# Delta-rule stage with weights in two split parts, and modulation rows loaded a step ahead of their sums

## The chip, the cores and the metric

The kernel runs on one core of one Trainium2 chip. The metric is the device time of one execution in microseconds (us), the median of several runs.

## What is computed

A sequence of 256 rows of 1024 float32 values goes through two blocks. The first is a state-space block whose normalizations are modulated by rows made from a vector `c`; the second has two layers, one with a gated delta rule and one with gated linear attention, each followed by an MLP. The parts that matter here, cut from the reference:

```python
def adaln(c, w, b):                       # twice: before the mixer and before the feed-forward
    mod = jax.nn.silu(c) @ w + b          # 3 x 1024 values each
    shift, scale, gate = jnp.split(mod, 3, axis=-1)

def _mixer_gdn(h, w_in, conv_w, a_log, dt_bias, norm_g, w_out):     # 8 heads of 128
    proj = jnp.matmul(h, w_in)            # columns: q, k, v, z (1024 each), beta and gate (32)
    qkv = silu(_depthwise_conv(proj[..., :A_CONV_CH], conv_w))      # 5 taps
    q, k = _l2norm(...), _l2norm(...)
    o_f = _gated_delta_chunked(q, k, v, beta[0], g[0])
    o_b = _flip(_gated_delta_chunked(_flip(q), _flip(k), _flip(v), _flip(beta[1]), _flip(g[1])))
    return jnp.matmul(_rmsnorm(o_f + o_b, norm_g) * silu(z), w_out)
```

## The kernel before, in words

All activations are float32. A weight matrix is cut into pieces of 128 x 1024 values (512 KB). SyncE's queue loads each into a buffer of the tag "raw" (six buffers), and `w3` brings it into one of three forms. In form "S" ScalarE writes the high part, rounded to float32r, and VectorE subtracts it from the piece for the low part. In form "D" ScalarE writes the negated rounded piece, a DMA from GpSimd's queue adds the piece to it, which leaves the low part, and ScalarE writes the high part. High and low parts lie in buffers of the tag "w" (eight, so four weights). A split weight takes three float32r products for each k (`mm3`: high by high, high by low, low by high). In form "N" the piece goes to TensorE unsplit, in one float32 product for each k, which the trace shows as two instructions. `self.form` is a string whose letters alternate over the weights: "SDND" in the state-space stage, "SD" for the gates, "S" in most others and "N" in the delta-rule stage (`gdn`). There every second weight is also loaded straight into a "w" buffer (`self.deep`).

The feed-forward before `gdn` ends with a normalization whose rows are transposed by TensorE and, for form "N", copied once into `h2` (`xpose`). `gdn` then runs, in the order of the program: the first half of z (`proj_z(0, True)`, four weights), `small_tok("w_ba")` (one weight, with the gate's softplus behind it), the k projections (`qkv(4 + i)`, two weights each, with a five-tap convolution whose other taps are VectorE's, line 555), the decay matrices (`decay`, whose right-hand sides `sr` also take "w" buffers), the Gram matrices `MT`, eight block copies by ScalarE (line 1199), a forward substitution of 31 steps on VectorE (lines 1255 and 1259), the placement of its result in `C` and `CT` (line 1272), two levels of block products (lines 1285 to 1304), the v and q projections, the products of the two directions (lines 1332 to 1421), and the second half of z (`proj_z(1, False)`). The next stage begins with `w_aout`.

The 48 modulation rows of `adaln` are sums on VectorE: each row of 128 x 1024 weights is loaded into a "raw" buffer and multiplied with `silu(c)` and summed in one instruction (line 452). Sixteen are made at the start. 24 wait in a list, from which `ada_next` takes one in each of four groups of the state-space stage, two after each of eight gate projections and one at each turn in `merge`; the last eight are made in the feed-forward.

The order on each engine is not the order of the program. A planner fixes each engine's instructions ahead of the run, from the program's order as priority and from its own times for when each is ready; buffers of one tag are handed out in turn. At run time each engine goes through its list in order. The 31-tap convolution of the state-space stage (`acc`) has a priority below all else.

Of the kernel before, what the change touches and what calls it, by code (L numbers as in the profile page):

```python
# [18 lines left out]
P = 128  # L19
T = 256  # L20
D = 1024
# [50 lines left out]
NW = 14  # L72
FORM_GDN = "N"

# [41 lines left out]
class K:  # L116
    def __init__(self, ctx, tc, A):
        self.tc, self.nc, self.A = tc, tc.nc, A
        pool = lambda name, **kw: ctx.enter_context(tc.tile_pool(name=name, **kw))
        self.cp = pool("cp", bufs=1)  # L120
        self.px = pool("px", bufs=1)
        self.dp = pool("dp", bufs=1, space=bass.MemoryType.DRAM)
        self.wp = pool("wp", bufs=1)
        self.wx = self.big = self.sm = self.ps = self.kp = None
        self.n = self.nw = 0
        self.pending = None
        self.form = "S"
        self.deep = False

# [31 lines left out]
    def w3(self, name, i, nk, extra=False):  # L161
# [4 lines left out]
        if form == "N":  # L166
            if self.deep and self.nw % 2:
                t = self.wp.tile([P, 1024], F32, tag="w", bufs=8, name=self.nm("wn"))
                nc.sync.dma_start(t, self.A[name][i])
            else:  # L170
                t = self.raw(self.A[name][i])
            return (t.rearrange("p (k c) -> p k c", k=nk),)
# [276 lines left out]
    def ada(self, name, i, mod):  # L449

        w = self.raw(self.A[name][i])
        self.nc.vector.tensor_tensor_reduce(  # L452
            out=w, in0=w, in1=self.sc, scale=1.0, scalar=0.0, op0=ALU.mult, op1=ALU.add,
            accum_out=mod[:, i : i + 1],
        )

    def ada_next(self, n):

        for a in self.waiting[:n]:
            self.ada(*a)  # L460
        del self.waiting[:n]
# [51 lines left out]
    def hsplit(self):  # L513
        t = self.px.tile([P, 2, 2, 8, P], F32R, tag="hh", name=self.nm("hh"))
        return t[:, 0], t[:, 1], None, t

    def h32(self):
        return self.px.tile([P, 2, 2, 8, P], F32, tag="hh", name=self.nm("h32"))[:, 0]

    def xpose(self, src, t, out):  # L520

        nc = self.nc
        for k0 in (0, 4):
            b = self.pS()
            for kk in range(4):
                nc.tensor.transpose(b[:, kk * P : (kk + 1) * P], src[:, (k0 + kk) * P : (k0 + kk + 1) * P], self.ident)
            nc.scalar.copy(out[:, t, k0 : k0 + 4, :], b.rearrange("p (k t) -> p k t", k=4))

# [80 lines left out]
    def state_space(self, h, banks):  # L609
# [70 lines left out]
        for g in range(4):  # L680
# [22 lines left out]
            def ev_z(b):  # L703
                for t in range(2):
                    self.silu2(z[:, t], b[t])

            self.proj_tok("w_z", g, h, ev_z)
            nc.vector.tensor_tensor(
                out=x0s.rearrange("p (h d) -> p h d", h=8),
# [82 lines left out]
    def merge(self, yT, acc, tg):  # L792
# [39 lines left out]
        for i in range(4):  # L832
            self.projA([("w_conv_out", i, ev_c(i))], ch)
            self.ada_next(ADA_PER[3])
        self.ada_next(24)
        self.ada_bias(self.mod2, "b_ada_ffn", 0, 16)
# [82 lines left out]
    def feed_forward(self, mh):  # L919
# [51 lines left out]
        nc.gpsimd.dma_start(wf, self.A["r_final"])  # L971
        h2 = self.h32()

        def norm2(t, b):
            self.residual(t, b, gate2[0])
            y = self.rms_tok(self.x[:, t], wf)
            self.later(t, lambda: self.xpose(y, t, h2))
            nc.gpsimd.dma_start(self.spill[:, t], y)

        self.down("w_ffn_down", 11, hidden, norm2)  # L980
        return None, None, h2

# [75 lines left out]
    def gdn(self, h):  # L1058
# [43 lines left out]

        self.form = FORM_GDN
        self.deep = True
        proj_z(0, True)
# [171 lines left out]
        for hq, l in ((0, 0), (0, 1), (1, 0), (1, 1)):  # L1277
            for t in range(2):
# [25 lines left out]
                nc.vector.copy_predicated(CT[:, gs], mask, wb.rearrange("p (h l) -> p h l", h=4))  # L1304

        for i in range(4):
            vv = self.smt([P, 2, T], "vT")
            qkv(8 + i, vv)
            to_tok(vt, vv, 2 * i)
# [22 lines left out]
        for hq in range(2):  # L1332
# [91 lines left out]
            for t in range(2):  # L1424
# [6 lines left out]
                for hh in range(4):  # L1431
# [3 lines left out]
                    )  # L1435
        self.deep = False
        return self.halves_out(zg)
# [375 lines left out]
```

## Time and profile before

| | |
|---|---|
| median of 3 runs | 1398.12 us |
| lowest and highest | 1397.02 and 1402.75 us |
| the profiled execution's own time | 1398.72 us |
| its span, first to last instruction | 1397.0 us |
| its mean granted TensorE clock | 0.979 |

The profile is one execution. Its rows give busy time, idle time and what ended the idle time (the releaser, inferred from semaphore events). PE is TensorE, PEld its weight loads, DVE VectorE, ACT ScalarE, POOL GpSimd, SP SyncE; L555 is line 555 of the kernel. Matmuls are pipelined, so a row's busy time is longer than the distance from one matmul to the next; distances are read from starts.

### The profile page before, as it was taken

How to read it: one execution, taken by the hardware profiler on the slowest of the kernel's cores; microseconds unless marked ns; L12 is line 12 of the kernel's file. 1: busy time of each engine (PE TensorE's matmuls, PEld its weight loads, DVE VectorE, ACT ScalarE, POOL GpSimd, SP SyncE). 2: the span in 40 equal slices, each digit the busy share in tenths (PEclk: the TensorE clock that was granted, in tenths of full speed). 3: DMA queues.
4: the chain of work that ended last, by engine and by line, in shares of the span. 5: the costliest groups of instructions: out<-in, count | busy, mean ns of one | idle time of the engine just before them, and what ended most of it. 6: DMA issues, size and time to landing. Idle time of an engine off the chain costs nothing. (4 is left out here: it accounts for less than half of the span.)

```text
span 1397.0 us, 19743 instructions
## 1 busy us (share of the span) xinstructions
PE 1308.5 (94%) x7336; PEld 1113.3 (80%) x7336; DVE 1000.3 (72%) x1890; ACT 732.9 (52%) x1309; POOL 98.6 (7%) x115
## 2 busy tenths in 40 slices
PE   5898999889998999998989898999999999899997
PEld 4797888789986888875877776788887987688886
DVE  7989988779467777744479976866575796866564
ACT  4655878655446544524344454555444655555450
POOL 0111101010000000000100531000000000000000
PEclk9999999999899999998999999999999999999999
DMA  9898577799355666535423014856464323676530
GB/s 337 289 258 223 172 199 201 226 297 349 104 199 177 235 220 213 192 151 169 136 69 106 31 61 160 265 193 208 130 205 149 122 71 114 207 238 201 179 122 30
DMA packets 69136, 251.69 MB, mean 180 GB/s; under 512 B 7951, under 2 KB 8079, under 8 KB 68528
## 3 DMA queue, kind: packets, MB, share of 16 engines
q1 hardware_dynamic: 62208, 224.08, 47.8%
q0 software_dynamic: 6832, 26.35, 8.2%
q8 instruction: 57, 0.93, 0.3%
q14 instruction: 39, 0.32, 0.1%
HBM read 232.06 MB, written 2.10 MB: 168 GB/s over the span
## 5 line engine op out<-in xcount | busy, mean ns | idle before, releaser
L185 DVE TENSOR_TENSOR wlo<-raw,whi 128x1024 fp32r<-128x1024 f32 (+1 forms) x200 | 241.2, 1211 | 75.9 <-ACT whi L184 71.8
L184 ACT CAST whi<-raw 128x1024 fp32r<-128x1024 f32 (+1 forms) x200 | 207.4, 1042 | 143.1 <-PE psa L201 42.0
L185 DVE TENSOR_TENSOR xlo<-raw,xhi 128x1024 fp32r<-128x1024 f32 x100 | 122.0, 1223 | 73.6 <-ACT xhi L184 69.7
L184 ACT CAST xhi<-raw 128x1024 fp32r<-128x1024 f32 x100 | 104.9, 1051 | 89.3 <-DMA raw<-in_w_mlp 66.8
L231 PE MATMUL psa<-hh,whi 128*128 128x512 f32 x384 | 136.9, 396 | 0.0
L231 PE MATMUL pss<-hh,whi 128*128 128x512 f32 x384 | 136.4, 396 | 0.0
L200 PE MATMUL psb<-xhi,hid 128*128 128x512 f32 x344 | 135.5, 394 | 0.6 <-ACT hid L375 0.6
L202 PE MATMUL psb<-xhi,hidl 128*128 128x512 f32 x344 | 135.8, 395 | 0.0
L201 PE MATMUL psb<-xlo,hid 128*128 128x512 f32 x344 | 135.5, 394 | 0.0
L202 PE MATMUL psa<-hh,wlo 128*128 128x256 f32 x432 | 125.3, 290 | 6.0 <-DMA wlo<-raw 6.0
L200 PE MATMUL psa<-hh,whi 128*128 128x256 f32 x432 | 126.5, 294 | 4.5 <-DVE c L555 2.5
L201 PE MATMUL psa<-hh,whi 128*128 128x256 f32 x432 | 124.8, 289 | 0.9 <-DVE hh L195 0.9
L232 PE MATMUL psa<-hh,wlo 128*128 128x256 f32 x384 | 107.2, 279 | 0.0
L232 PE MATMUL pss<-hh,wlo 128*128 128x256 f32 x384 | 107.0, 279 | 0.0
L555 DVE SCALAR_TENSOR_TENSOR acc<-u,vecs,acc 128x240 f32<-128x240 f32 (+25 forms) x240 | 100.9, 464 | 0.3
L202 PEld LDWEIGHTS psa<-hh,wlo 128*128 128x128 f32 x432 | 84.7, 196 | 7.6 <-DMA wlo<-raw 6.8
L200 PEld LDWEIGHTS psa<-hh,whi 128*128 128x128 f32 x432 | 84.8, 196 | 6.9 <-ACT hh L194 2.9
L201 PEld LDWEIGHTS psa<-hh,whi 128*128 128x128 f32 x432 | 84.6, 196 | 2.5 <-DVE hh L195 1.9
L231 PEld LDWEIGHTS pss<-hh,whi 128*128 128x128 f32 x384 | 72.1, 188 | 17.1
L231 PEld LDWEIGHTS psa<-hh,whi 128*128 128x128 f32 x384 | 72.0, 188 | 17.0
L452 DVE CUSTOM_DVE_ANT_0 raw<-raw,g 128x1024 f32<-128x1024 f32 x48 | 58.6, 1221 | 30.9 <-DMA raw<-in_w_ada_ffn 18.8
L200 PEld LDWEIGHTS psb<-xhi,hid 128*128 128x128 f32 x344 | 64.4, 187 | 16.6 <-ACT hid L375 1.2
(426 smaller groups left out, 2944.6 us busy)
## 6 DMA issues: line engine op xcount, KB each, us to landing
raw<-in_w_mlp SPq DMA_DIRECT2D x120, 512.0 KB, 4.5
raw<-in_w_ffn_in SPq DMA_DIRECT2D x40, 512.0 KB, 4.4
wlo<-raw POOLq DMA_DIRECT2D x31, 512.0 KB, 6.8
raw<-in_w_ada_mix SPq DMA_DIRECT2D x24, 512.0 KB, 5.3
raw<-in_w_ada_ffn SPq DMA_DIRECT2D x24, 512.0 KB, 4.4
raw<-in_w_ffn_down SPq DMA_DIRECT2D x22, 512.0 KB, 4.4
raw<-in_w_xs SPq DMA_DIRECT2D x16, 512.0 KB, 4.6
raw<-in_w_z SPq DMA_DIRECT2D x16, 512.0 KB, 5.5
```

The costliest lines, as they stand in the source:

```text
L184: nc.scalar.copy(hi, t)
L185: nc.vector.tensor_tensor(out=lo, in0=t, in1=hi.bitcast(F32), op=ALU.subtract)
L200: mm(out, ah, bh, start=start, stop=False)
L201: mm(out, ah, bl, start=False, stop=False)
L202: mm(out, al, bh, start=False, stop=stop)
L231: mm(b, wh[:, k], x[3][:, :, :, k], start=k == 0, stop=False, skip_group_check=True)
L232: mm(b[:, T:], wl[:, k], x[0][:, :, k], start=False, stop=k == 7, skip_group_check=True)
L452: self.nc.vector.tensor_tensor_reduce(out=w, in0=w, in1=self.sc, scale=1.0, scalar=0.0, op0=ALU.mult, op1=ALU.add, accum_out=mod[:, i : i ...
L555: nc.vector.scalar_tensor_tensor(out=o, in0=i, scalar=taps[:, j : j + 1], in1=o, op0=ALU.mult, op1=ALU.add)
```

## The change

In the delta-rule stage the form "N" with its deep loads is gone. Up to the block products the form is "S"; from the v projections on it is "D". As the second half of z is emitted after v and q, its weights are "D" too. The normalized rows ahead of the stage are split into two parts (`xpose_split`), because the split products need them. `ada_next` now sums the rows that the call before it loaded, and then loads the next ones; calls with 0 sum what is loaded and load nothing. The helpers `h32` and `xpose` go.

```diff
--- before.py
+++ after.py
@@ -70,7 +70,7 @@
 FORM_GATES = "SD"
 
 NW = 14
-FORM_GDN = "N"
+FORM_GDN = ("S", "D")
 
 
 def m_lev(l):
@@ -123,9 +123,9 @@
         self.wp = pool("wp", bufs=1)
         self.wx = self.big = self.sm = self.ps = self.kp = None
         self.n = self.nw = 0
+        self.loaded = []
         self.pending = None
         self.form = "S"
-        self.deep = False
 
     def phase(self, name, big, wx, a, b, s):
         return _Phase(self, name, big, wx, a, b, s)
@@ -164,11 +164,7 @@
         self.nw += 1
         form = self.form[self.nw % len(self.form)] if self.nw > NW else "S"
         if form == "N":
-            if self.deep and self.nw % 2:
-                t = self.wp.tile([P, 1024], F32, tag="w", bufs=8, name=self.nm("wn"))
-                nc.sync.dma_start(t, self.A[name][i])
-            else:
-                t = self.raw(self.A[name][i])
+            t = self.raw(self.A[name][i])
             return (t.rearrange("p (k c) -> p k c", k=nk),)
         if extra and self.wx is not None:
             hi, lo = (self.wx.tile([P, 1024], F32R, tag="wx", name=self.nm(v)) for v in ("xhi", "xlo"))
@@ -448,7 +444,9 @@
 
     def ada(self, name, i, mod):
 
-        w = self.raw(self.A[name][i])
+        self.ada_sum(self.raw(self.A[name][i]), i, mod)
+
+    def ada_sum(self, w, i, mod):
         self.nc.vector.tensor_tensor_reduce(
             out=w, in0=w, in1=self.sc, scale=1.0, scalar=0.0, op0=ALU.mult, op1=ALU.add,
             accum_out=mod[:, i : i + 1],
@@ -456,8 +454,9 @@
 
     def ada_next(self, n):
 
-        for a in self.waiting[:n]:
-            self.ada(*a)
+        for a in self.loaded:
+            self.ada_sum(*a)
+        self.loaded = [(self.raw(self.A[name][i]), i, mod) for name, i, mod in self.waiting[:n]]
         del self.waiting[:n]
 
     def ada_bias(self, mod, bname, lo, hi):
@@ -513,18 +512,6 @@
     def hsplit(self):
         t = self.px.tile([P, 2, 2, 8, P], F32R, tag="hh", name=self.nm("hh"))
         return t[:, 0], t[:, 1], None, t
-
-    def h32(self):
-        return self.px.tile([P, 2, 2, 8, P], F32, tag="hh", name=self.nm("h32"))[:, 0]
-
-    def xpose(self, src, t, out):
-
-        nc = self.nc
-        for k0 in (0, 4):
-            b = self.pS()
-            for kk in range(4):
-                nc.tensor.transpose(b[:, kk * P : (kk + 1) * P], src[:, (k0 + kk) * P : (k0 + kk + 1) * P], self.ident)
-            nc.scalar.copy(out[:, t, k0 : k0 + 4, :], b.rearrange("p (k t) -> p k t", k=4))
 
     def xt(self):
         return self.px.tile([P, 2, D], F32, tag="x", name=self.nm("x"))
@@ -705,6 +692,7 @@
                     self.silu2(z[:, t], b[t])
 
             self.proj_tok("w_z", g, h, ev_z)
+            self.ada_next(0)
             nc.vector.tensor_tensor(
                 out=x0s.rearrange("p (h d) -> p h d", h=8),
                 in0=xdt[:, 0].rearrange("p (h d) -> p h d", h=8),
@@ -832,7 +820,8 @@
         for i in range(4):
             self.projA([("w_conv_out", i, ev_c(i))], ch)
             self.ada_next(ADA_PER[3])
-        self.ada_next(24)
+        assert not self.waiting
+        self.ada_next(0)
         self.ada_bias(self.mod2, "b_ada_ffn", 0, 16)
         self.ada_bias(self.mod, "b_ada_mix", 16, 24)
         self.gate1 = self.gate_rows(self.mod, 0.5)
@@ -969,16 +958,16 @@
 
         wf = self.g4()
         nc.gpsimd.dma_start(wf, self.A["r_final"])
-        h2 = self.h32()
+        h2 = self.hsplit()
 
         def norm2(t, b):
             self.residual(t, b, gate2[0])
             y = self.rms_tok(self.x[:, t], wf)
-            self.later(t, lambda: self.xpose(y, t, h2))
+            self.later(t, lambda: self.xpose_split(y, t, h2[0], h2[1]))
             nc.gpsimd.dma_start(self.spill[:, t], y)
 
         self.down("w_ffn_down", 11, hidden, norm2)
-        return None, None, h2
+        return h2
 
 
     def layer_norm(self, gname, i, last=False):
@@ -1100,8 +1089,7 @@
 
             self.proj_tok("w_az", c, h, ev_z, early)
 
-        self.form = FORM_GDN
-        self.deep = True
+        self.form = FORM_GDN[0]
         proj_z(0, True)
         kT = self.bigt([P, 8, T], name="kT")
         qT = self.bigt([P, 8, T], name="qT")
@@ -1303,6 +1291,7 @@
                     nc.tensor.matmul(wb[:, j * P : (j + 1) * P], U[:, j], R2[:, j], start=True, stop=True)
                 nc.vector.copy_predicated(CT[:, gs], mask, wb.rearrange("p (h l) -> p h l", h=4))
 
+        self.form = FORM_GDN[1]
         for i in range(4):
             vv = self.smt([P, 2, T], "vT")
             qkv(8 + i, vv)
@@ -1433,7 +1422,6 @@
                     nc.vector.scalar_tensor_tensor(
                         out=o, in0=o_all[:, t, h0 + hh], scalar=rs[:, hh : hh + 1], in1=o, op0=ALU.mult, op1=ALU.mult
                     )
-        self.deep = False
         return self.halves_out(zg)
 
     def halves_out(self, zg):
```

## Rows read from the trace of the kernel before

**Rows 1.** The page's first part: busy us, share of the span and number of instructions of each engine.

```profile
PE 1308.5 (94%) x7336; PEld 1113.3 (80%) x7336; DVE 1000.3 (72%) x1890; ACT 732.9 (52%) x1309; POOL 98.6 (7%) x115
```

**Rows 2.** Busy time in stretches of the delta-rule stage: window, its length, then PE, PEld, DVE, ACT and POOL busy us with instruction counts, granted TensorE clock, DMA share, GB/s.

```profile
624.00:640.00 16.00, 15.76 (x45) 7.67 (x45) 4.34 (x7) 2.60 (x7) 1.68 (x3) 1.00 0.31 100
640.00:666.00 26.00, 22.31 (x89) 16.62 (x88) 15.31 (x62) 15.88 (x48) 0.00 (x0) 0.81 0.56 189
666.00:703.00 37.00, 35.07 (x191) 30.55 (x191) 15.93 (x46) 14.94 (x27) 7.57 (x6) 1.00 0.35 120
703.00:770.00 67.00, 60.61 (x271) 50.06 (x269) 59.03 (x151) 28.29 (x47) 3.12 (x4) 0.95 0.28 87
770.00:802.00 32.00, 28.59 (x202) 24.61 (x203) 30.00 (x46) 14.45 (x43) 16.28 (x12) 0.95 0.11 34
802.00:847.00 45.00, 41.54 (x290) 35.34 (x289) 30.15 (x69) 26.64 (x87) 14.42 (x14) 1.00 0.18 59
```

**Rows 3.** The timeline of TensorE, in four pairs: split products of 512 columns, split products of 256 columns (in each pair the third product of one k and of the next), unsplit z products (two k of one weight in each row, two instructions for each k), unsplit qkv products (one weight in each row). Columns: start us, us, engine, line, operation, output and input, columns, count.

```profile
213.15 0.39 PE L202 MATMUL psa<-whi,hh 128*128 128x512 f32 x1
213.83 0.39 PE L202 MATMUL psa<-whi,hh 128*128 128x512 f32 x1
...
290.81 0.28 PE L202 MATMUL psa<-hh,wlo 128*128 128x256 f32 x1
291.17 0.28 PE L202 MATMUL psa<-hh,wlo 128*128 128x256 f32 x1
...
624.50 1.88 PE L248 MATMUL psa<-raw,h 128*128 128x512 f32 x4
626.22 1.88 PE L248 MATMUL psa<-wn,h 128*128 128x512 f32 x4
...
670.15 3.62 PE L209 MATMUL psa<-h,raw 128*128 128x256 f32 x16
673.60 3.62 PE L209 MATMUL psa<-h,wn 128*128 128x256 f32 x16
```

**Rows 4.** What a split costs. First the page's groups of form "S" (busy us, mean ns, idle before), then for form "D" ScalarE's first pass (line 180), GpSimd's issue of the adding DMA (line 181), both least, median and most in ns, and its time from issue to landing, and one convolution's eight taps on VectorE from the timeline.

```profile
L185 DVE TENSOR_TENSOR wlo<-raw,whi 128x1024 fp32r<-128x1024 f32 (+1 forms) x200 | 241.2, 1211 | 75.9 <-ACT whi L184 71.8
L184 ACT CAST whi<-raw 128x1024 fp32r<-128x1024 f32 (+1 forms) x200 | 207.4, 1042 | 143.1 <-PE psa L201 42.0
...
L180 ACT ACTIVATE wlo<-raw x31: 1040/1056/1067, 58.6 to 307.6; 128x1024 fp32r<-128x1024 f32 x31
...
L181 POOL DMA_DIRECT2D wlo<-raw x31: 859/869/977, 60.0 to 308.9; - x31
...
DMA to landing us min/median/max: 4.5/6.8/10.6
...
674.96 3.25 DVE L555 SCALAR_TENSOR_TENSOR c<-kT,vecs,c 128x254 f32<-128x254 f32 x8 [5.72 <-ACT c L548]
```

**Rows 5.** The stretch from the block copies to the end of the stage: rows of the timeline (with the idle time before, and what ended it, in brackets), and three of VectorE's groups from 703 to 802.

```profile
704.37 4.69 ACT L1199 COPY g<-MT 32x256 f32<-32x256 f32 x8 [3.32 <-DVE MT L1186]
715.25 0.20 DVE L1255 TENSOR_TENSOR tm<-g,g 128x31 f32<-128x31 f32 x1
726.33 0.48 DVE L555 SCALAR_TENSOR_TENSOR c<-vT,vecs,c 128x254 f32<-128x254 f32 x1 [2.10 <-ACT c L548]
766.11 4.10 DVE L1272 TENSOR_TENSOR CT<-g,g 32x512 f32<-32x512 f32 x4
816.41 1.02 PE L248 MATMUL psa<-raw,h 128*128 128x512 f32 x2
...
L555 DVE SCALAR_TENSOR_TENSOR c<-qT,vecs,c 128x255 f32<-128x255 f32 x16 | 9.7, 613 | 0.0
L555 DVE SCALAR_TENSOR_TENSOR c<-vT,vecs,c 128x255 f32<-128x255 f32 x16 | 7.7, 480 | 0.0
L185 DVE TENSOR_TENSOR wlo<-raw,whi 128x1024 fp32r<-128x1024 f32 x3 | 3.7, 1220 | 0.0
```

**Rows 6.** Two modulation sums and the TensorE instructions that were held (timeline), and the windows that follow (columns as in rows 2).

```profile
203.54 1.23 DVE L452 CUSTOM_DVE_ANT_0 raw<-raw,g 128x1024 f32<-128x1024 f32 x1 [2.90 <-issue]
206.13 1.08 PE L691 MATMUL pss<-ident,xsT 128*128 128x128 f32 x4 [2.95 <-DVE xsT L568]
205.00:210.00 5.00, 3.87 (x11) 2.77 (x12) 4.71 (x12) 1.57 (x3) 0.00 (x0) 0.66 0.35 105
...
260.27 1.23 DVE L452 CUSTOM_DVE_ANT_0 raw<-raw,g 128x1024 f32<-128x1024 f32 x1 [3.10 <-DMA raw<-in_w_ada_ffn]
264.35 1.97 PE L741 MATMUL psb<-xdt,E 128*128 128x64 f32 x8 [3.35 <-DVE E L736]
265.00:270.00 5.00, 5.00 (x25) 4.90 (x24) 3.42 (x6) 2.90 (x10) 0.00 (x0) 0.50 0.44 169
```

**Rows 7.** DMA and queues in the stages with form "D": an adding DMA's issue and the TensorE product that waited for it (timeline), the two DMA queues from 110 to 180 us (packets, MB, share of 16 engines), and a wait of SyncE's queue from 220 to 340 us (us in total, times, longest).

```profile
286.86 0.86 POOL L181 DMA_DIRECT2D wlo<-raw  x1 [6.43 <-ACT wlo L180]
297.46 0.49 PE L202 MATMUL psa<-hh,wlo 128*128 128x256 f32 x1 [3.61 <-DMA wlo<-raw]
...
q1 hardware_dynamic: 2748, 10.01, 39.4%
q0 software_dynamic: 1096, 3.99, 31.2%
...
SPq L158 <- DVE mod L452: 24.5, 13, 6.1
```

## The prediction, made before the changed kernel ran

> **What bounds the kernel now.** I read first the busy time of the engines [rows 1]: TensorE 94%, VectorE 72%, ScalarE 52% of a span of 1397.0 us. These are averages; the change touches two places, so next I read the stages around them [rows 2]. In the delta-rule stage TensorE is busy 35.07 of 37 us while the k projections run (666 to 703) and VectorE 15.93: there a shorter product is a shorter stage. From 703 to 802 VectorE is busy 89 of 99 us with the 31-step substitution and the conv taps of v and q, and TensorE's v and q products run under it. From 640 to 666 neither is full: the decay matrices wait for ScalarE.
>
> The products themselves come next [rows 3]. One w_qkv weight unsplit is 16 instructions in 3.45 us (start to start). Three products of a split weight take 0.36 us per k at 256 columns, 2.88 us per weight, and 0.68 us per k at 512 columns against 0.86 us (1.72 us for two). So TensorE gets shorter by 0.57 us per qkv or ba weight, 25 of them, and by 0.18 us for each of 32 z products: 14.3 + 5.8 = 20.1 us of work. The question is how much of it lies on the path.
>
> Last the modulation rows [rows 6]. VectorE stands 2.90 and 3.10 us for a row that has not landed, with its queue behind it. Both times TensorE then stands for what was queued there, 2.95 and 3.35 us, and in the next 5 us its granted clock is 0.66 and 0.50 (0.50 is 1.2 of 2.4 GHz): 1.7 and 2.5 us more.
>
> **The change part by part.** The sum is made against the profiled execution's own 1398.72 us (span 1397.0); the median of the runs shown is 0.6 us lower.
>
> *z(0).* Two halves of 6.9 us (eight products of 0.86) shrink to 5.4: 2.9 us, on the path. The second half needs its transposes split into two parts now, and a subtraction on VectorE (half the columns of the 1.21 us one [rows 4], 0.6 or 0.7 us) comes before its third product; the rows of that half are ready no earlier than before. Between 1.4 (only one half counts) and 2.9; I take 1.9.
>
> *ba, k0, k1.* Three weights by 0.57: 1.7 us, ahead of everything in the stage. Their splits (1.05 us ScalarE, 1.21 us VectorE each [rows 4]) lie under the end of the down projection and z, where VectorE is busy 4.34 of 16 us [rows 2]; without that cover they would cost up to 2.3 us each.
>
> *Decay stretch.* k2 to k5 share the eight "w" tiles with the decay's right-hand sides, so their splits fall where ScalarE is busy 15.88 of 26 us and TensorE's granted clock falls to 0.81 [rows 2]. Nothing to 4.2 us (four casts, all in series) is lost; I take 1.5, since the products of k2 come after the decays anyway.
>
> *k2 to k7.* Six by 0.57 is 3.4 us. But a pair now costs VectorE 3.25 us of taps and 2.4 of two splits [rows 4], 5.65 us before its silu and the decayed grams, against 5.8 us of products on TensorE before its transposes, norms and grams. The two come near level; between nothing and 3.4, I take 2.0.
>
> *v and q.* Sixteen weights by 0.57 is 9.1 us, put at nothing: VectorE's substitution and taps cover it, from 715.25 until CT is written at 770.2 [rows 5]. If VectorE were not full, all 9.1 would count. On the cost side each weight now wants 2.1 us more of ScalarE, a GpSimd issue of 0.87 us and a DMA that adds [rows 4]. ScalarE is busy 28.29 of 67 us there [rows 2]; 16 weights add 33.4 and fill it to 92%, in order, with the conv's first taps behind the casts. The eight "w" tiles hold four weights, so a weight has three products, 8.6 us, from its free tiles to its turn; 1.05 us of cast and about 0.3 of handover leave 7.2 for the DMA. Its landing is 4.5, 6.8, 10.6 us (least, median, most). The 16 DMA engines spend 2.87 us on each such transfer (31.2% of 70 us for 3.99 MB, times 0.524 MB) and 1.44 on a plain load (39.4% for 10.01 MB) [rows 7]: 4.3 us per weight, about the present pace of 67 us for 16. GpSimd's queue holds nothing long, but an issue placed behind a norm's power waits for VectorE. From nothing to 26 us (first rival); I take 3.0, nearer to nothing, because four weights are split ahead while k runs.
>
> The Trainium skill, page "DMA: Bandwidth & Descriptors", section "Anatomy of one DMA", gives a GpSimd-issued DMA 2.0 us plus bytes at 436 GB/s, which by that is an estimate of 3.2 us for 512 KB. By it no weight would be late, the 3.0 us would be nothing and the sum 1384.5; the trace's median of 6.8 us disagrees for the adding transfer, and the sum goes by the trace.
>
> *The splits of w_aout.* Before, free "w" tiles let three of them run inside the VectorE-bound stretch, 1.22 us each, 3.7 in all [rows 5]. Now the tiles are taken until z(1) is done, so they move behind 802, where VectorE is busy 30.15 of 45 us. Between nothing and 3.7; I take 2.5, two of the three, as that stretch still has 10 us of idle.
>
> *z(1).* It fills TensorE's gaps until 816.41 [rows 5], beside the chain of small products. It gets 2.9 us shorter and, since v and q end earlier, part of it can run before 770. Between nothing and 8.6 us (ten pieces of 0.86 leaving the chain); I take 2.5, because the chain also waits for VectorE, busy 30 of 32 us.
>
> *The modulation sums.* The loads stay where they are; the sum is emitted one step later, and its row buffer, one of six, is held a step longer. If the waits go, the two stalls and the slow clock after them go: 10.5 us [rows 6]. If the planner, which takes what it believes is ready, puts the sum in the same place, nothing. I take 5.0. The removed final flush issues nothing, as the 24 rows are used up before it.
>
> Sum: 1.9 + 1.7 - 1.5 + 2.0 - 3.0 + 2.5 + 2.5 + 5.0 = 11.1 us, so 1387.6 us.
>
> **The rivals.** About 7 us, 0.5%, is what a measurement of this kernel tells from no change.
>
> *A late low part stalls VectorE.* Place: the v and q projections, 697 to 770. The conv taps stand in VectorE's order between substitution steps, so a late product holds the substitution too. It decides once the adding DMA lands later than the 7.2 us worked out above. For it: one landing, issued at 286.86, took 10.6 us where the DMA engines were full, and TensorE stood 3.61 us [rows 7]; before, VectorE stood 2.10 us at 726.33 for such a tap [rows 5]. Against it: the median landing, 6.8 us, is under 7.2 [rows 4]. At 2.1 us of wait and 1.2 of slow clock for each of eight pairs it costs 26 instead of 3.0: 1411. Chance 0.15.
>
> *The gain is hidden.* VectorE sets the end of the stage and the sums stay where they are. Then only z(0), ba, k0, k1 and the k pairs count, 1.9 + 1.7 + 2.0 - 1.5, and the adding DMA costs nothing: 4.1 us, 1394.6. For it: the 89 of 99 us. Against it: the w_aout splits leave that stretch. Chance 0.22.
>
> *The later sums hold the loads.* SyncE already stands 24.5 us for sums from 220 to 340 [rows 7]. If each of the eight steps is held 1.3 us longer, a sum's own length, that is 10.4 us lost instead of 5.0 gained: 1403.0. Against it: a sum is ready work, and VectorE has idle there. Chance 0.06.
>
> *GpSimd's issues are held by VectorE.* In the stretch 770 to 802 the two already stretch each other: a conv tap of q, beside GpSimd's R2t products, takes 0.58 to 0.61 us where one of v takes 0.48 [rows 5]. Were each issue held by a VectorE instruction of 1.2 us, the landing would go to 8.0, 0.8 over the 7.2, a quarter of it per weight with four in flight: 4 us over 20 weights, 1391.6. Against it: 31 issues lie between 0.859 and 0.977 us beside a busy VectorE [rows 4]. Chance 0.05. The Trainium skill, page "SBUF — State Buffer", section "SBUF: two separate sides", states this rule: a DMA from GpSimd's queue cannot have its descriptors written while VectorE runs in a two-port mode; this trace's issue times show none of it.
>
> **How the numbers follow.** The forecast, 1387.6, has 0.52. Its own range is 1373 to 1391: it reaches 14 us down if sums and z(1) give their full 10.5 and 8.6 and the adding DMA costs 0.5, and 3.5 up if the sums give 1.5. Chances of the signs: faster by over 0.5% (below 1391.1) the forecast and a tenth of the hidden case, 0.54; within 0.5% the rest of that case and the held issues, 0.25; slower, the late low part and the held loads, 0.21. The range that leaves out 2 in 10 cuts the worst of the late low part and the very best: 1371 to 1406 (the low end 2 us under that range, for waits not counted here).
>
> **What would show it.** In the changed profile: qkv weights at 2.88 us per 24 products from 640 on; the first substitution step 4 us earlier than 715.25; VectorE's idle between 709 and 770 no more than now; no w_aout subtraction there; z(1) ending before 816; no row wait above 2 us ahead of a sum, and no half clock near 205 and 265. I am wrong if TensorE waits for the adding DMA in v and q for more than 3 us in all, if ScalarE's casts hold the block copies at 704.37 (4.69 us, all on the way to VectorE), or if the sums wait as long as before.

## The result and the profile after

The changed kernel took 1412.03 us (median of 12 runs, 1406.15 to 1418.83) against 1399.63 for the kernel before: ratio 1.010, 95% interval 1.0081 to 1.0119. (Two of the twelve executions of the kernel before were slow, 1838.32 and 3277.51 us, and the ratio leaves them out.) That is 1.0% slower, where 1387.6 (1371 to 1406) was forecast. The profiled execution is the longest of the twelve, 1418.83 us with a span of 1417.1. Part of that is no effect of the change: until shortly before the delta-rule stage both programs issue the same instructions in the same order (VectorE's first 895, to 599 us in the kernel before, TensorE's first 3477, to 606, SyncE's first 228 loads, to 590), and with that same order z(0)'s first product came anywhere between 619.0 and 627.4 us in eleven profiles of this study. So times of the stage are taken from its own marks.

The page's first part [rows 1]:

```profile
PE 1307.0 (92%) x7568; PEld 1133.7 (80%) x7568; DVE 1019.6 (72%) x1907; ACT 782.0 (55%) x1362; POOL 116.7 (8%) x135
```

TensorE is busy as long as before, in a longer span. The stretches of [rows 2] in the changed kernel, columns as there:

```profile
624.00:640.00 16.00, 15.76 (x73) 12.62 (x72) 8.35 (x12) 5.84 (x11) 1.69 (x3) 1.00 0.22 69
640.00:666.00 26.00, 21.67 (x116) 17.10 (x114) 16.04 (x63) 16.03 (x48) 0.00 (x0) 0.74 0.15 54
666.00:703.00 37.00, 32.88 (x246) 31.83 (x246) 21.11 (x46) 26.27 (x39) 10.40 (x9) 0.91 0.62 171
703.00:770.00 67.00, 54.05 (x380) 51.54 (x379) 49.78 (x143) 51.97 (x75) 16.26 (x19) 0.90 0.95 223
770.00:802.00 32.00, 24.64 (x136) 21.38 (x136) 26.04 (x33) 13.37 (x27) 7.86 (x7) 0.89 0.44 130
802.00:847.00 45.00, 36.13 (x272) 33.05 (x270) 36.47 (x70) 24.77 (x83) 22.33 (x18) 0.96 0.13 45
```

Against [rows 2], the two engines that were near full from 703 to 770 are emptier: TensorE fell from 60.61 to 54.05, VectorE from 59.03 to 49.78 of 67 us. ScalarE rose from 28.29 to 51.97 us with the casts, and the DMA engines from 0.28 to 0.95. Before that, from 640 to 666, the DMA engines fell from 0.56 to 0.15. The same view in steps of 4 us:

```profile
652.00:656.00 4.00, 2.44 (x4) 1.00 (x4) 3.67 (x13) 3.57 (x12) 0.00 (x0) 0.50 0.00 0
...
664.00:668.00 4.00, 3.01 (x16) 2.52 (x15) 0.29 (x2) 2.31 (x3) 1.21 (x2) 0.79 0.00 0
...
672.00:676.00 4.00, 4.00 (x20) 4.00 (x20) 1.65 (x3) 1.04 (x1) 0.00 (x0) 0.51 0.88 311
676.00:680.00 4.00, 4.00 (x36) 4.00 (x35) 1.80 (x2) 1.74 (x3) 0.00 (x0) 1.00 0.73 278
...
744.00:748.00 4.00, 4.00 (x23) 4.00 (x23) 4.00 (x12) 0.33 (x1) 0.86 (x1) 0.57 1.05 258
```

While the decays run (652) nothing is loaded and TensorE is at half clock (0.50). The clock comes back for a moment (0.79 from 664 to 668), falls again while TensorE stands 2.14 us for the first low part of k2 (until 669.92), and is back at 676. At 744 the DMA engines are full, and TensorE is at half clock once more, after a wait of 3.48 us for a low part.

VectorE's timeline, with the idle time before an instruction and what ended it: the first substitution step, the three waits inside the substitution and behind it, and the end of CT.

```profile
722.00 0.20 DVE L1243 TENSOR_TENSOR tm<-g,g 128x31 f32<-128x31 f32 x1
...
735.67 0.48 DVE L542 SCALAR_TENSOR_TENSOR c<-vT,vecs,c 128x254 f32<-128x254 f32 x1 [3.81 <-ACT c L535]
...
755.91 0.69 DVE L555 SCALAR_TENSOR_TENSOR qT<-th,c 128x512 f32<-128x512 f32 x1 [5.06 <-ACT th L554]
...
773.56 0.16 DVE L1125 TENSOR_SCALAR rsq<-pss 128x4 f32<-128x4 f32 x1 [4.21 <-PE pss L1121]
...
780.04 4.19 DVE L1260 TENSOR_TENSOR CT<-g,g 32x512 f32<-32x512 f32 x4
```

VectorE, which set the end of this stretch, stands 13.1 us in three places; before, its wait at such a tap was 2.10 us [rows 5]. From the first substitution step to the end of CT, columns as in [rows 2], before and after:

```profile
715.25:770.21 54.96, 48.83 (x216) 40.03 (x216) 51.05 (x128) 19.71 (x32) 2.02 (x2) 0.94 0.25 77
```
```profile
722.00:784.23 62.23, 49.05 (x314) 45.07 (x314) 46.75 (x122) 39.49 (x53) 13.55 (x15) 0.92 0.92 228
```

VectorE is idle 15.5 us of it instead of 3.9, and has 4.3 us less to do. ScalarE and TensorE are named as the releasers, but they wait themselves. The waits of TensorE from 640 to 800 (us in total, times, longest), then those of SyncE's queue, before and after:

```profile
PE psa L198 <- DMA wlo<-raw: 11.9, 6, 3.5
```
```profile
SPq L158 <- PE psa L209: 85.4, 12, 13.8
```
```profile
SPq L158 <- DMA wlo<-raw: 90.3, 20, 8.7
```

Twenty times a load could not be issued until an adding DMA had finished with its row buffer. The queue stood about as long before, but then for TensorE's products. What the two queues moved from 660 to 800 (packets, MB, share of 16 engines), and the adding DMA from issue to landing:

```profile
q0 software_dynamic: 2880, 10.49, 40.4%
q1 hardware_dynamic: 4032, 14.68, 30.5%
```
```profile
DMA to landing us min/median/max: 4.6/7.0/11.5
```

20 adding DMAs took 40.4% of 140 us, 2.83 us of all 16 engines each; 28 loads took 30.5%, 1.53 each. Together that is 99 us of engine time in the 117 us between 668, when the first splits free their rows, and 785, a mean share of 0.85. Of the 20 adding DMAs 8 landed later than 7.2 us, all of them issued from 735 on.

The stage by its marks, worked out from the timelines (z(0): its first product to beta's first; then from beta's first product to the first substitution step; from there to the end of CT; from there to the first output transposes on TensorE), for all kernels with changes in this stage, and what the ratio is worth in us of 1399. The marks that [rows 3], [rows 5] and the rows above do not show are beta's first product and the output transposes of the kernel before, and z(0)'s first product, beta's and the transposes of after:

```profile
639.62 3.62 PE L209 MATMUL pss<-h,raw 128*128 128x256 f32 x16
825.73 0.59 PE L367 MATMUL pss<-ident,x 128*128 128x128 f32 x2 [1.21 <-DVE x L1433]
```
```profile
627.37 0.39 PE L196 MATMUL psa<-whi,hh 128*128 128x512 f32 x1
639.92 0.28 PE L196 MATMUL pss<-hh,whi 128*128 128x256 f32 x1
843.50 0.59 PE L363 MATMUL pss<-ident,x 128*128 128x128 f32 x2 [1.00 <-DVE x L1422]
```

| kernel | z(0) | to step 1 | to CT | to transposes | sum against before | by the ratio |
|---|---|---|---|---|---|---|
| before | 15.1 | 75.6 | 55.0 | 55.5 | | |
| after | 12.5 | 82.1 | 62.2 | 59.3 | +14.9 | +14.0 |
| e1, half adds | 12.6 | 81.9 | 55.9 | 62.4 | +11.6 | +12.3 |
| e2, only z(0), beta, k split | 12.6 | 80.8 | 53.1 | 55.8 | +1.1 | +1.3 |
| e3, all split by VectorE | 12.6 | 83.6 | 60.0 | 57.9 | +12.9 | +12.5 |
| e4, decays in own tiles | 12.6 | 78.7 | 57.3 | 58.6 | +6.0 | +4.6 |
| e5, z(1) unsplit | 12.6 | 81.4 | 62.9 | 56.6 | +12.3 | +10.4 |
| e6, no early w_aout | 12.6 | 82.1 | 62.6 | 56.8 | +12.9 | +17.8 |
| e7, GpSimd subtracts | 12.6 | 94.3 | 77.2 | 57.7 | +40.6 | +40.4 |
| e8, before with own tiles | 15.1 | 68.5 | 52.9 | 57.8 | -6.9 | -6.9 |
| e10, e2 with own tiles | 12.6 | 73.0 | 50.6 | 58.5 | -6.5 | -7.6 |

But for e6, which pays 7.4 us behind the last mark, the marks (of one execution each) account for each ratio to within 2 us.

### The profile page after: what moved, and what is told of

Read it like the earlier page. It is cut to its first block, busy times and chain, and to the rows that moved or that the text cites. A ratio compares the mean times of both kernels' runs of the same rounds, so it can differ in the third digit from the quotient of the medians.

```text
span 1417.1 us, 20354 instructions
## 1 busy us (share of the span) xinstructions
PE 1307.0 (92%) x7568; PEld 1133.7 (80%) x7568; DVE 1019.6 (72%) x1907; ACT 782.0 (55%) x1362; POOL 116.7 (8%) x135
## 5 line engine op out<-in xcount | busy, mean ns | idle before, releaser
L181 DVE TENSOR_TENSOR wlo<-raw,whi 128x1024 fp32r<-128x1024 f32 (+1 forms) x213 | 257.6, 1214 | 87.9 <-ACT whi L180 84.0
L180 ACT CAST whi<-raw 128x1024 fp32r<-128x1024 f32 (+1 forms) x213 | 220.6, 1043 | 157.2 <-PE psa L197 49.8
L198 PE MATMUL psa<-hh,wlo 128*128 128x256 f32 x624 | 185.0, 296 | 18.1 <-DMA wlo<-raw 15.9
L196 PE MATMUL psa<-hh,whi 128*128 128x256 f32 x624 | 185.5, 298 | 8.8 <-DVE c L542 6.0
L197 PE MATMUL psa<-hh,whi 128*128 128x256 f32 x624 | 184.1, 295 | 1.1 <-DVE hh L191 1.1
L198 PEld LDWEIGHTS psa<-hh,wlo 128*128 128x128 f32 x624 | 126.3, 202 | 21.4 <-DMA wlo<-raw 18.2
L196 PEld LDWEIGHTS psa<-hh,whi 128*128 128x128 f32 x624 | 126.2, 202 | 11.4 <-issue 6.2
L197 PEld LDWEIGHTS psa<-hh,whi 128*128 128x128 f32 x624 | 126.1, 202 | 2.9 <-DVE hh L191 2.3
L228 PE MATMUL psa<-hh,wlo 128*128 128x256 f32 x384 | 107.8, 281 | 0.0
L196 PE MATMUL psa<-whi,hh 128*128 128x512 f32 x192 | 79.9, 416 | 6.6 <-ACT hh L190 3.5
L227 PEld LDWEIGHTS psa<-hh,whi 128*128 128x128 f32 x384 | 72.0, 187 | 16.2
L450 DVE CUSTOM_DVE_ANT_0 raw<-raw,g 128x1024 f32<-128x1024 f32 x48 | 58.5, 1221 | 34.3 <-DMA raw<-in_w_ada_ffn 21.0
```

What stands on the lines that cost most here:

```text
L180: nc.scalar.copy(hi, t)
L181: nc.vector.tensor_tensor(out=lo, in0=t, in1=hi.bitcast(F32), op=ALU.subtract)
L196: mm(out, ah, bh, start=start, stop=False)
L197: mm(out, ah, bl, start=False, stop=False)
L198: mm(out, al, bh, start=False, stop=stop)
L227: mm(b, wh[:, k], x[3][:, :, :, k], start=k == 0, stop=False, skip_group_check=True)
```

## Experiments

The diffs are cut to the lines that carry the edit. Two theories stand first. A: the adding DMAs keep the 16 engines full, and rows, and with them low parts, come late. B: ScalarE's fixed order makes the low parts late. C adds to either: the decays hold the w tiles, so nothing is split or loaded from 648 to 668.

**Half of each adding DMA (e1).**

```
-            nc.gpsimd.dma_start(out=lo, in_=t, accum_op=ALU.add)
+            n = t.shape[-1] // 2 if self.half else t.shape[-1]
+            nc.gpsimd.dma_start(out=lo[:, :n], in_=t[:, :n], accum_op=ALU.add)
```

> As after, but the adding DMA of v, q and the second z half carries only the first 512 of 1024 columns; the low parts of the other columns are left wrong. ScalarE, GpSimd, VectorE and TensorE do the same work. Theory A (the 16 DMA engines are full from 684 to 776 us, and adding transfers take twice a load's time there): 20 x 1.44 = 29 us of engine time go, the waits of VectorE for a q or v product (13 us in three places) go nearly all, 1399 to 1402 us, ratio to before about 1.00. Theory B (ScalarE's fixed order makes the low parts late: its casts stand behind copies that wait for TensorE): the waits stay, 1410 to 1413 us, ratio 1.008 to 1.01.

Measured: 1411.13 us, ratio 1.0088 (1.0058 to 1.0118), no different from after. Taken alone the ratio speaks for B. The marks do not: from step 1 to CT 55.9 us instead of 62.2, where A expected the waits to go, and from CT to the transposes 62.4 instead of 59.3. Its windows from step 1 to CT and from behind CT, its two queues from 660 to 800, and the half transfers from issue to landing:

```profile
715.91:771.81 55.90, 45.48 (x313) 41.82 (x311) 47.93 (x126) 40.67 (x54) 13.64 (x15) 0.97 0.79 193
...
813.40:823.80 10.40, 8.53 (x36) 7.94 (x37) 6.55 (x15) 4.17 (x13) 1.79 (x2) 0.50 0.01 2
```
```profile
q1 hardware_dynamic: 4320, 15.73, 36.4%
q0 software_dynamic: 2880, 5.24, 21.9%
```
```profile
DMA to landing us min/median/max: 3.3/5.0/7.0
```

With ScalarE's work the same (40.67 us, 39.49 in after), the DMA share falls from 0.92 to 0.79, no half transfer lands later than 7.0 us, and VectorE's idle time falls from 15.5 to 8.0 us (3.9 before). So halving the adding DMAs takes back 7.5 of the 11.6 us that it rose, and A holds for the larger part of it; whether the rest is their other half or ScalarE's order (B) this run does not tell. Of the 6 us, 3 are given back behind CT, where TensorE runs at half clock (0.50) for 10 us. Why the stretch behind CT is longer, here and in after, is what e5 and e6 ask.

**Only z(0), beta and k split (e2).**

```
-FORM_GDN = ("S", "D")
+FORM_GDN = ("S", "N")
```

> z(0), beta and k split by VectorE as in after; v, q and z(1) unsplit as before, from six raw and the w tiles. The unsplit products read only the rounded high part of the layer's input, so the output is slightly off; the time is that of the exact product. Theory of the forecast (z(0) 1.9, ba and k0, k1 1.7, decay stretch -1.5, k2 to k7 2.0): 4 us faster than before, 1395, ratio 0.997. Rival C (the k weights cannot be split until the decay matrices give their w tiles back, so the first substitution step comes 4 us late, as in the trace of after): 1402 to 1404, ratio 1.002 to 1.004. Either way the three waits of VectorE between 731 and 774 are gone.

Measured: 1401.09 us, 1.0009 (0.9989 to 1.0028). The three waits are gone (53.1 us to CT). Step 1 comes 5.2 us later than before and z(0) is 2.6 shorter: the split of k costs what the split of z(0) brings. C's place is right, its price for the whole too high, and the forecast's gain of 4 is not there.

**v, q and z(1) split by VectorE (e3).**

```
-FORM_GDN = ("S", "D")
+FORM_GDN = ("S", "S")
```

> As after, with v, q and the second z half split by VectorE too: no adding DMA at all. Theory A: the DMA share falls to about 0.5, no product waits for a DMA, but VectorE takes 16 x 1.22 = 19.5 us more in a stretch where it has 10 idle in 99, and the second z half 4.9: 1412 to 1418 us, ratio 1.009 to 1.014. If the adding DMA were the only thing that cost and VectorE had room: 1400 to 1403.

Measured: 1411.89 us, 1.0089 (1.0062 to 1.0117), just under the lower edge of what was expected. VectorE's busy time from 703 to 802, and what TensorE waits for:

```profile
703.00:802.00 99.00, 72.25 (x523) 66.90 (x522) 93.54 (x199) 51.12 (x87) 13.04 (x11) 0.88 0.32 101
```
```profile
PE pss L1136 <- DVE vT L555: 8.9, 3, 5.3
```

VectorE is busy 93.54 of 99 us, and now TensorE waits for it. The change's way of sparing VectorE and the plain way cost the same.

**The decays' right-hand sides in tiles of their own (e4).**

```
+        sr = [self.bigt([P, 2, 1024], F32R, "sr") for _ in range(2)]
...
-                r = self.wp.tile([P, 1024], F32R, tag="w", bufs=8, name=self.nm("sr"))
+                r = sr[t][:, d]
```

> As after, with the decays' right-hand sides in two of the stage's big tiles instead of the eight w tiles; nothing else is changed. Theory C (the w tiles keep casts and loads out of 648 to 668, DMA is idle there, k2 runs 6 us late and at half clock, and the loads are crowded into the adding DMAs' time): the DMA engines work from 648 on, k2 starts in the decay stretch, 6 us of k and about half of the 13 us of waits are won back: 1398 to 1403, ratio 1.000 to 1.003. Theory A alone (the adding DMAs fill the engines whatever comes before): only the 4 to 6 us of k, 1406 to 1408, ratio 1.005. If the decay tiles cost nothing: 1412.

Measured: 1403.88 us, 1.0033 (1.0007 to 1.0059), just above C's range; by its time alone, A's 1.005 lies within the interval too. By the marks both parts of C come in part: step 1 is 3.4 us earlier, and from there to CT it is 4.9 us shorter. The transposes of k2 and k3 come 33.8 us after beta's first product instead of 45.3. One detail was wrong. The 20 us from 8.1 us behind beta's first product, in after and in e4:

```profile
648.00:668.00 20.00, 14.68 (x56) 10.03 (x55) 10.95 (x46) 16.64 (x46) 1.21 (x2) 0.66 0.00 0
```
```profile
642.40:662.40 20.00, 19.75 (x149) 18.64 (x149) 13.98 (x55) 17.52 (x48) 0.35 (x1) 1.00 0.17 58
```

The DMA engines hardly work there in e4 either (0.17). What is won is that the splits of k2 and k3 no longer wait for the decays, and that TensorE has products between them: it is busy 19.75 us instead of 14.68, at a clock of 1.00 instead of 0.66. Part of the slow clock only moves: behind this window, from 662.4 to 678.4, e4's clock is 0.68.

**z(1) unsplit (e5) and no early w_aout (e6).**

```
             if hq == 1:
+                self.form = "N"
                 proj_z(1, False)
```

> As after, with the second z half unsplit again (it reads only the rounded high part of the layer's input, so the output is slightly off; the time is that of the exact product). In the half-add run the substitution ended 5 us earlier than in after and the chain behind it, from the end of CT to the first output transposes, took 62.4 us where before has 55.5 (after: 59.3). Theory F (the z(1) products were what kept TensorE busy, at its full clock, under that chain; split, with their weights ready early, they are done before it starts): that stretch goes back to 55 to 57 us at a granted clock of 0.95 or more, and with four adding DMAs fewer the whole is 1404 to 1408, ratio 1.003 to 1.006. Rival G (the stretch is longer for the three or four w_aout splits that VectorE now makes in it): it stays at 58 to 60, 1408 to 1412.

```
-        k.down("w_aout", 4, k.pairs(oT), ln, pre=PRE, first=1)
+        k.down("w_aout", 4, k.pairs(oT), ln, pre=0, first=1)
```

> As after, with no w_aout weight split before the next stage has begun (they take that stage's own tiles). Rival G: VectorE has 5 us less work between the end of CT and the output transposes, the stretch falls from 59.3 to 55 or 56 us; the next stage's first products then wait for their splits, so the whole may be no faster. Theory F: the stretch stays at 58 to 60 us.

Measured: e5 1410.50 us, 1.0074 (1.0047 to 1.01); e6 1417.37, 1.0127 (1.0092 to 1.0162). Both stretches fell below 57 us. By the length of the stretch alone e5 bears F out; its whole time lies in G's range, and its profile speaks against F. The stretch in after, in e5 and in e6:

```profile
784.20:843.50 59.30, 46.89 (x337) 43.58 (x337) 49.64 (x81) 30.67 (x96) 27.11 (x21) 0.91 0.16 50
```
```profile
781.90:838.50 56.60, 45.55 (x337) 43.00 (x337) 46.42 (x73) 27.47 (x92) 27.34 (x21) 0.91 0.11 33
```
```profile
777.80:834.70 56.90, 43.17 (x337) 40.46 (x337) 46.50 (x77) 27.87 (x93) 27.08 (x21) 0.97 0.05 15
```

TensorE has the same 337 instructions in all three (z(1) is done before CT in e5 as well) and in e5 the same clock, 0.91. So it is not z(1) under the chain that shortened the stretch; what it would bring if it did run there, e5 does not show. What both runs took out is VectorE's work, 3.2 and 3.1 us: four w_aout splits in after, two in e5 and none in e6, and in e5 eight taps of q instead of fourteen. That is G, and the stretch of before, with two splits, has VectorE at 46.93. e5's substitution did not shorten (62.9), but its contents changed:

```profile
719.02:781.91 62.89, 49.85 (x298) 40.79 (x298) 50.57 (x130) 35.58 (x49) 9.86 (x11) 0.95 0.80 210
```

VectorE's idle time fell from 15.5 to 12.3 us with four adding DMAs fewer, while two w_aout splits and six taps of q moved in from behind CT: the work moved from one stretch to the other. In e6 the next stage pays 7.4 us for its late splits.

**GpSimd subtracts (e7), in e4.**

```
-            nc.vector.tensor_tensor(out=lo, in0=t, in1=hi.bitcast(F32), op=ALU.subtract)
+            eng = nc.gpsimd if form == "P" else nc.vector
+            eng.tensor_tensor(out=lo, in0=t, in1=hi.bitcast(F32), op=ALU.subtract)
```

> As the run with the decays in their own tiles (ratio 1.0033), with the low parts of v, q and the second z half subtracted by GpSimd, as ScalarE's cast and one GpSimd instruction, instead of by an adding DMA. GpSimd's products of 512 columns take 1.31 us, so 1024 should take 2.6 and the 20 of them 52 us, in some 100 us. Theory A (full DMA engines): the DMA share from 684 to 776 falls from 0.85 to 0.3, no product waits for a DMA, ScalarE has 21 us less to do: ratio 0.995 to 1.000. Rival: VectorE's taps and steps are stretched beside GpSimd as q's taps were in before (0.48 to 0.61 us), a fifth of 60 us: 1408 to 1415, ratio 1.006 to 1.011.

Measured: 1439.73 us, 1.0289 (1.0252 to 1.0325): the rival, at more than twice its price. GpSimd's subtractions from 640 to 860 and VectorE's taps of v from 703 to 802:

```profile
L182 POOL TENSOR_TENSOR wlo<-raw,whi 128x1024 fp32r<-128x1024 f32 x20 | 53.5, 2677 | 32.8 <-ACT whi L180 32.4 <-PE psa L199 0.4
...
L543 DVE SCALAR_TENSOR_TENSOR c<-vT,vecs,c 128x254 f32<-128x254 f32 (+1 forms) x32 | 27.3, 873 | 0.0
```

A subtraction takes 2.68 us, close to the estimate of 2.6. A tap of v takes 0.873 us in the mean where it took 0.480 [rows 5], but no tap takes that: 26 of the 32 take 0.44 to 0.48 us, and six take 2.58 to 2.64, each of them beside a subtraction. One such tap on VectorE, and the subtraction on GpSimd:

```profile
735.67 2.60 DVE L543 SCALAR_TENSOR_TENSOR c<-vT,vecs,c 128x255 f32<-128x255 f32 x1
```
```profile
735.13 2.87 POOL L182 TENSOR_TENSOR wlo<-raw,whi 128x1024 fp32r<-128x1024 f32 x1 [1.67 <-ACT whi L180]
```

They end within 0.3 us of each other: the tap does not run slowly, it is held. The Trainium skill, page "SBUF — State Buffer", section "Who interferes with whom", says that a VectorE instruction with two SBUF inputs contends with a GpSimd instruction that reads SBUF, and that what they share is an exclusive lock; this trace agrees, with the six taps of 2.58 to 2.64 us.

**The kernel before, with the decays in own tiles (e8).** The diff is e4's, on the kernel before.

> The kernel before, with the decays' right-hand sides in two of the stage's big tiles: the w tiles are free for the unsplit k weights, and their products can run between the decays, where TensorE stood 3.6 us and ran at half clock for 10. Expected from that: the first substitution step 3 to 6 us earlier, and as VectorE sets the end from there, all of it kept: 1394 to 1397, ratio 0.996 to 0.998. If VectorE's taps of k2 and k3, which come earlier too, push the decays' own VectorE half back: no change, 1.000.

Measured: 1392.38 us, 0.9951 (0.9928 to 0.9974): faster than both kernels. Its first window after beta:

```profile
648.00:668.00 20.00, 20.00 (x105) 17.21 (x103) 12.67 (x53) 15.50 (x46) 0.00 (x0) 1.00 0.35 107
```

TensorE is busy all 20 us (16.31 before, clock 0.74), step 1 comes 7.1 us earlier, and the whole is 6.9 us shorter.

**The sums held in program order (e9).** In after, the sums stand where they stood in the kernel before: all of them lie in the part whose order did not change. This run is the kernel before with the modulation half of the change, and it holds the sums where the change writes them:

```
+        if pin:
+            self.tc.keep_in_program_order(ins)
...
+        for a in self.loaded:
+            self.ada_sum(*a, pin=True)
```

> The kernel before, with the modulation half of the change and one thing more: the 24 sums that wait for the gates and the convolution are held at their place in the program, so that VectorE's order really changes (as the change stands it does not: the orders of all engines are the same as before's). Loads are issued in the same order. Forecast's term: the waits of 2.9 to 3.2 us ahead of the sums at 105, 203 and 260 go, with the 2.5 to 3.4 us that TensorE stood for each and the slow clock after them; 5 us taken, 10.5 at most: 1389 to 1395, ratio 0.993 to 0.997. Rival (later sums hold the loads: their row buffers, two or more of six, come free a step later, and a held sum in program order holds what stands behind it): 1402 to 1406, ratio 1.002 to 1.005.

Measured: 1410.31 us, 1.0095 (1.0061 to 1.013): slower as the rival said, and dearer. Waits ahead of the sums over the whole run (before: 18.8 us in 12 times for these rows, and 12.0 in others), what TensorE waited for most from 60 to 400 (before: 6.0 us in 4 times for the same DMA), and SyncE's queue there, for sums, before and in e9:

```profile
  DMA raw<-in_w_ada_ffn: 6.4, 6
```
```profile
PE psa L203 <- DMA wlo<-raw: 17.2, 6, 5.2
```
```profile
SPq L158 <- DVE mod L452: 37.1, 16, 6.5
```
```profile
SPq L159 <- DVE mod L455: 14.2, 14, 1.5
```

The waits of the held sums went as hoped (the six that are left lie in the feed-forward), but TensorE stands 17.2 us for low parts. The rival's reason, that sums hold the loads, is not what the queue shows: it stood less for sums than before. Why the low parts came later stays open.

**e2 with the decays in own tiles (e10).**

> The run with only z(0), beta and k split, with the decays in their own tiles (the unsplit products read only the rounded high part of the input, times are those of the exact ones). It stands to the run of before with own tiles (ratio 0.9951) by the split of z(0), beta and k alone. If the w tiles of the decays were what made the split of k a loss, TensorE's 5.2 us shorter products and z(0)'s 2.5 now show: ratio 0.991 to 0.995. If the split itself is the loss (casts of ScalarE in the decay stretch, where it is busy 15 of 20 us, and two subtractions for a pair of weights on VectorE between taps and grams), the first substitution step comes 77 to 79 us after the first beta product instead of 68.5: ratio 0.998 to 1.001.

Measured: 1389.67 us, 0.9946 (0.9924 to 0.9968), at the edge of the first range, but level with e8: neither forecast came. z(0) is 2.5 us shorter, step 1 4.5 later, the substitution 2.3 shorter. The transposes of k2 and k3 come 33.8 us after beta's first product in both, those of k4 and k5 12.4 us after them instead of 7.0: the casts and subtractions of k4 and k5 lie behind the decays and the taps in ScalarE's and VectorE's order. So with the tiles out of the way the split of z(0), beta and k is worth nothing either way. Of e4's delay to step 1 (78.7) 5.7 us come with v, q and z(1) split: between 685 and 700 ScalarE casts for v ahead of k's last block copies.

Four ratios make a square: k split or not, by v, q and z(1) unsplit, 1.0009 and 1 with shared tiles, 0.9946 and 0.9951 with own; v, q and z(1) split on top, 1.0100 and 1.0033. The split of z(0), beta and k changes the time by 1.3 us with shared tiles and by -0.7 with own, both within the intervals; that of v, q and z(1) costs 12 to 13 in both.

## Why the prediction was wrong

*What bounds the kernel* was read rightly: VectorE sets the end from step 1 on (e3), and a shorter product counts for little. The step that failed is the one on v and q. Its own sign of being wrong came: TensorE waited 11.9 us for adding DMAs, where 3 was the limit. Step by step:

- *z(0)*, 1.9 forecast: 2.6 measured. *ba, k0, k1*, 1.7: beta's first product to the first decay product went from 11.6 to 10.0 us, 1.6.
- *Decay stretch*, 1.5 lost: mis-sized. The transposes of k2 and k3 came 5.2 us later instead of 1.6 earlier, 6.8 lost. The step saw four casts that fall into the stretch and priced the casts. It missed that in after they wait for the last decay, with their subtractions behind them, so that TensorE waits 2.1 us and runs at 1.2 GHz again until 676 (0.51 in the window from 672). The tiles are only the place of this loss, not its whole cause: with own tiles (e10 against e8) the split of k still brings step 1 4.5 us later, one pair further on.
- *k2 to k7*, 2.0 gained: the next two pairs took 20.25 us, 20.05 before, and the rest to step 1 took 1.1 more. It was said that TensorE and VectorE come near level there; level means no gain.
- *v and q*, 3.0 lost: the stretch from step 1 to CT became 7.3 us longer, with 11.6 us more of VectorE's idle time and 4.3 less of its work. This is the step that failed in its method. It worked out 4.3 us of engine time per weight, called that "about the present pace", and then judged by a single landing (6.8 against 7.2 us). The median landing did stay at 7.0. But 20 adds, 20 loads for them and 8 of w_aout fill the engines, 20 of the loads wait for an add, and from 735 on 8 adds landed later than 7.2 us, up to 11.5. A resource at its pace's limit is a bound, not a cover.
- *The splits of w_aout*, 2.5 gained: they did not move out of VectorE's way but into the chain. Three lay before 776, two of them before CT, and one at 814; now four lie between 788 and 803. The two before CT are part of the 4.3 us above, and two more lie behind it. *z(1)*, 2.5 gained: its products did leave the chain, all of them, and the chain did not shorten; as far as e5 and e6 show, its length follows VectorE's work. The working gave that as the reason for taking 2.5 of 8.6, and it was reason for nothing. Behind CT 3.8 were lost.
- *Modulation sums*, 5.0 gained: nothing. The working named the case ("if the planner puts the sum in the same place, nothing") and gave it a chance only inside a rival, *The gain is hidden* (0.22). Two of the sums in after, each between the same two instructions as in before (VectorE's timeline):

```profile
206.24 1.23 DVE L450 CUSTOM_DVE_ANT_0 raw<-raw,g 128x1024 f32<-128x1024 f32 x1 [3.29 <-issue]
262.72 1.23 DVE L450 CUSTOM_DVE_ANT_0 raw<-raw,g 128x1024 f32<-128x1024 f32 x1 [2.65 <-DMA raw<-in_w_ada_ffn]
```

The waits are close to those of [rows 6], 2.90 and 3.10.

Two readings were off. z(1) does not end at 816.41 but with an eleventh pair at 822.41, and the first of the two sums is not shown to have waited for its row: its wait is put down to "issue". Both terms were wrong for other reasons.

Of the rivals, the late low part named the right mechanism and place (VectorE held between substitution steps by a late tap) at 26 us for 11.6; that its 1411 is close to 1412 is chance, as the forecast's gains were missing at the same time. *The gain is hidden* had both its conditions right, but took the adding DMA as free. The later sums did not come in after; e9, which moved them, was slower, but not by the waits that the rival named. GpSimd's issues were not held: in after the 20 took 0.853, 0.862 and 0.929 us (least, median, most). The estimate of 3.2 us for such a transfer, worked out from the Trainium skill's page "DMA: Bandwidth & Descriptors", section "Anatomy of one DMA", stays below every landing of the full ones (4.6 at least).

What stays open: what the 4.1 us are that VectorE stands in e1's substitution beyond before's. Why TensorE ran those 10 us of e1 at half clock behind CT: just before, it stood 2.96 us for VectorE (until 813.76), with no z(1) products left to fill such gaps as before has them until 822, but e6 has none either and a clock of 0.97. And why e8 is 2.3 us longer there than before: VectorE is busy 49.46 us instead of 46.93.

## What to carry to other kernels

Where an edit adds transfers, sum their engine time over the stretch with everything that must pass in it, before looking at one transfer's latency; work that is moved from a full engine to the DMA queues is free only while these have room, and a buffer that a transfer reads stays taken until it lands. When a planner sets the order, first see whether an edit changes that order at all. Temporaries that share buffers with a stream of weights stop the stream: giving the decays their own tiles brought more (6.9 us) than any split here. And a window that is compared between two runs is laid by marks of the program, not by the clock time: the same 20 us lay 5.6 us apart in after and e4.

## What the runs showed of the hardware

An adding DMA within SBUF takes the 16 engines 2.83 us for 512 KB, 1.85 times a plain load of that size in the same stretch (1.53; 1.70 in e1, 36.4% of 140 us by 30); half of one takes 1.53 (21.9% of 140 us by 20). A tap of VectorE beside a GpSimd subtraction takes either its own 0.48 us or, held by it, 2.58 to 2.64, while issuing adding DMAs from GpSimd beside a busy VectorE cost nothing that the issue times show. And the same order of instructions takes a different time to the same mark from execution to execution, 619.0 to 627.4 us here, more than most single edits of this study are worth: marks within the stage were needed to see them.
